# A second buffer for the convolved x, B and C tile in the projection phase of a hybrid attention/SSD layer

## The chip, the cores and the metric

The kernel runs on one core of a Trainium2 chip. The metric is the device time of one execution in microseconds (us), as the median of several runs. Before the change it is 2937.35 us, the median of 3 runs that lie between 2936.06 and 2943.05 us.

## What is computed

One step of a streaming encoder layer, for 2048 new prompt frames and 32 frames of a running stream. Only the mixer matters here. It projects the normalised input once, and reads attention (q, k, v) and a Mamba-2 SSD branch (z, x/B/C, dt) out of that projection:

```python
proj = h @ p['w_in']                      # q, k, v, z, xbc, dt_raw
xbc_c, conv_new = causal_dwconv(xbc, conv_prev, p['ssm_conv_w'], p['ssm_conv_b'])   # width 4
xbc_c = jax.nn.silu(xbc_c)
# x, B, C are parts of xbc_c
y, h_fin = ssd_scan(xh, dt, a, bm, cm, ssm_h0)
y = y + d_skip[:, None] * xh
y = rmsnorm(y * jax.nn.silu(z), p['g_ssm_out'])
out = jnp.concatenate([rmsnorm(attn, p['g_attn_out']), y], axis=-1) @ p['w_out']
```

A gated feed-forward network with a causal convolution of its own follows. Everything is float32 in and out; the matrix products are made from split operands (a high and a low part, three products).

## The kernel before

The features lie on the 128 partitions and the tokens along a row. The tokens are cut into four blocks (`SBS`): three of 512, and one of 544 that ends with the 32 frames of the running stream. The kernel has three parts: `phase_in` (phase one: all projections, the convolution and the SSD scan, block by block), then the attention, in which a stream of other work is interleaved with the heads, and with it the output projection and the feed-forward network.

One block `s` of phase one does, in the order of the source:

1. The normalised input is split into `xhi` and `xlo` (L315 to L323).
2. For each of the six column groups `c` of x, B and C (4 and 5 first, then 0 to 3), 24 matmuls (L161, by `dense`) fill a PSUM bank `o`, ScalarE copies it into the tile `raw` (L377, and L379 for the last 32 columns of the last block), and VectorE convolves it into the tile `xc`: one multiply-add with the bias (L384), three more taps (L388), then a sigmoid on ScalarE (L392) and a multiplication (L393).
3. The v projection (L412): 8 groups of 24 matmuls of 260 columns, whose banks ScalarE copies out into `v` (L419 in block 0, L421 after it). It needs no `xc`.
4. dt and its decays (L443 to L471), which go through memory once (`acD`) to be broadcast.
5. The SSD scan over 128 tokens at a time (L473 to L566). It reads `xc` as x, B and C and writes its result y over the x part of `xc` (L542, L545).
6. The next block's input is loaded and normalised (`prep`, L294 to L313), and k and q are projected (L573 to L594).
7. `gate` (L609) projects z and multiplies `xc` by silu(z) (L628, L630); `gate_norm` (L635) squares and sums `xc`, makes its reciprocal root (L180, L183), scales `xc` with it (L650), splits it into `khi` (L654, ScalarE) and `klo` (L656, GpSimd) and stores both. For the last block, steps 7 are not run here but as part of the stream beside the first attention heads.

So `xc` is taken at the head of a block and last read by L656 at the end of the block's step 7. Its pool `ssd_out` (opened in `build`, L1491) has one buffer, which the four blocks use in turn. The tile holds 6 x 547 float32 per partition, 13,128 bytes. `raw`, the input of the convolution, also has one buffer; the PSUM banks `o` (`psum_o`) are two, and the v projection, the x/B/C columns, k, q and z all use them.

Weights are made ready by `weight`: a DMA brings a piece (`wraw`), ScalarE writes its high part (L145), GpSimd subtracts that from it for the low part (L146). In phase one a piece is a whole group of 24 matmuls, and there are two buffers for it.

The order of the instructions on each engine isn't the source's. The framework (`schedule_with_timeline_sim=True`, L1616) orders them when the kernel is built: on a simulated time line, an engine takes the earliest instruction of the source whose inputs and buffers are ready by then. The order is then fixed. On the chip each engine works through its list, and an instruction that waits holds up what stands behind it on its engine.

Of the kernel before, what the change touches and what calls it, by code (L numbers as in the profile page):

```python
# [8 lines left out]
F32 = mybir.dt.float32  # L9
# [22 lines left out]
P = 128  # L32
# [220 lines left out]
def phase_in(kn, ctx):  # L253
# [101 lines left out]
    for s, (t0, nt) in enumerate(SBS):  # L355
# [5 lines left out]
            xs = split(s, nxt)  # L361
        xhi, xlo = xs
        raw = ep.tile([P, 6, 550], F32, name="raw")
        xc = kn.xcp.tile([P, 6, 547], F32, name="xc")
        W = 547 if last else 512
        nc.vector.tensor_copy(raw[:, :, 0:3], hist[:])
        if last:
# [233 lines left out]
        bufs = {"khi": 2, "klo": 2, "t": 2, "sq": 1}  # L601
# [870 lines left out]
def build(nc, tc, a, o):  # L1472
    kn = Kernel(nc, tc, a, o)
    with ExitStack() as ctx:
# [17 lines left out]
        with ExitStack() as c2:  # L1492
            kn.wp, kn.unit, kn.wbufs, kn.rbufs = c2.enter_context(tc.tile_pool(name="weights_in", bufs=1)), KC, 2, 2
            rest = phase_in(kn, c2)
# [125 lines left out]
```

## Time and profile before

| | |
|---|---|
| median of 3 runs | 2937.35 us |
| the profiled execution | 2941.02 us |
| its span (first to last instruction) | 2939.2 us |
| PE (TensorE matmul) busy | 2814.1 us, 96% of the span |
| DVE (VectorE) | 1690.8 us, 58% |
| ACT (ScalarE) | 1263.4 us, 43% |
| POOL (GpSimd) | 1275.4 us, 43% |
| granted TensorE clock, mean | 0.982 |
| first and last convolution step (L384) | 38.1 and 534.7 us from the span's start |

Names in a row of the profile are those of the program: `o L161` is the instruction of line 161 that writes a tile named `o`, and `out<-in` says what it writes and reads. PEld is TensorE's weight load, which overlaps the matmuls. In a list of waits, "A <- B: total, times, longest" says for how long A's engine sat idle until B released it. In a timeline, a row has its start and its length in us, the engine, the line, the operation, and how many instructions were merged; the bracket behind it is the idle time before it and what ended that.

### The profile page before, as it was taken

The numbers are of one execution on the slowest core, as the hardware profiler recorded it, in microseconds if no ns is written. First come the engines' busy times: TensorE is split into PE (matmuls) and PEld (weight loads), VectorE is DVE, ScalarE is ACT, GpSimd is POOL, SyncE is SP. The second block draws the span as 40 slices with busy tenths as digits, with TensorE's granted clock in tenths as the row PEclk, the third lists the DMA queues.
The fourth block names the chain that finished last, engine by engine and source line by source line (L and its number), as shares of the span: only waits on it lengthen the run. The fifth ranks groups of instructions, "written<-read, shape, count | busy, mean of one in ns | idle before, by whom it ended". The sixth has DMA issues, their size and how long they took to land.

```text
span 2939.2 us, 46252 instructions
## 1 busy us (share of the span) xinstructions
PE 2814.1 (96%) x16771; PEld 2427.5 (83%) x16771; DVE 1690.8 (58%) x2628; ACT 1263.4 (43%) x2622; POOL 1275.4 (43%) x1131
## 2 busy tenths in 40 slices
PE   7999999989889999999999999999999999999997
PEld 6777777977788888897788888977888889999997
DVE  7667586566773555447555556675666653623333
ACT  4344444337665555446333444654444443321111
POOL 4565555435766666656322323453223233511113
PEclk9999999989999999999999999999999999999999
DMA  5646464648787778777655556656555445765556
GB/s 179 183 137 193 132 176 124 174 115 271 247 282 263 253 263 276 266 256 250 215 180 172 174 180 219 225 182 205 176 172 170 160 159 202 241 181 179 170 178 200
DMA packets 333093, 586.47 MB, mean 200 GB/s; under 512 B 73306, under 2 KB 192738, under 8 KB 332866
## 3 DMA queue, kind: packets, MB, share of 16 engines
q1 hardware_dynamic: 332866, 583.52, 62.1%
q8 instruction: 134, 2.20, 0.3%
q14 instruction: 93, 0.76, 0.1%
HBM read 445.70 MB, written 137.69 MB: 198 GB/s over the span
## 4 chain that ended last, share of the span: by engine, by line
PE 72%; DVE 13%; DMA 7%; ACT 3%; issue 2%; POOL 1%; SPq 1%; DVEq 0%; ACTq 0%; POOLq 0%
PE o L161 35%; PE u L161 12%; PE t L161 10%; PE z L863 4%; PE pa L904 4%; PE pt L882 3%; DVE xc L388 2%; DMA acB<-acD 2%; PE o L412 1%; DVE acB L488 1%; DVE prow L714 1%; DMA xr<-hS 1%; DVE xc L384 1%; DVE xlo L320 1%; DVE x L310 1%
## 5 line engine op out<-in xcount | busy, mean ns | idle before, releaser
L161 PE MATMUL o<-xhi,w 128*128 128x512 f32 (+2 forms) x3968 | 1047.9, 346 | 24.1 <-ACT xhi L334 8.0
L161 PEld LDWEIGHTS o<-xhi,w 128*128 128x128 f32 x3968 | 697.3, 191 | 119.0 <-ACT xhi L334 8.0
L161 PE MATMUL o<-xlo,w 128*128 128x512 f32 (+2 forms) x1984 | 683.8, 345 | 6.3 <-DVE xlo L320 4.2
L146 POOL TENSOR_TENSOR w<-wraw,w 128x512 fp32r<-128x512 f32 (+3 forms) x244 | 384.3, 1577 | 261.4 <-ACT w L145 232.2
L719 POOL TENSOR_TENSOR beta<-beta,prow 128x512 f32<-128x512 f32 (+3 forms) x256 | 252.5, 987 | 442.7 <-DVE prow L714 366.8
L161 PEld LDWEIGHTS o<-xlo,w 128*128 128x128 f32 x1984 | 380.0, 192 | 50.4 <-DVE xlo L320 6.1
L161 PE MATMUL u<-xhi,w 128*128 128x512 f32 x1056 | 350.3, 398 | 0.0
L161 PE MATMUL o<-ah,w 128*128 128x512 f32 x992 | 344.4, 403 | 4.3 <-DVE f L1348 3.8
L1300 POOL TENSOR_TENSOR y<-y,gb 128x512 f32<-128x512 f32 (+1 forms) x88 | 116.0, 1318 | 503.2 <-ACT gb L1299 503.1
L714 DVE TENSOR_TENSOR_SCAN prow<-gam,prow,z 128x513 f32<-128x513 f32 x192 | 245.2, 1278 | 74.1 <-ACT beta L712 69.7
L887 DVE TENSOR_TENSOR wt<-pt,wt 128x512 fp32r<-128x512 f32 (+2 forms) x320 | 191.0, 602 | 159.6 <-ACT wt L886 157.8
L886 ACT CAST wt<-pt 128x512 fp32r<-128x512 f32 (+2 forms) x320 | 166.9, 527 | 218.2 <-PE pt L882 216.3
L145 ACT CAST w<-wraw 128x512 fp32r<-128x512 f32 (+3 forms) x244 | 172.1, 705 | 170.6 <-PE o L161 98.6
L161 PEld LDWEIGHTS u<-xhi,w 128*128 128x128 f32 x1056 | 199.1, 189 | 46.8
L161 PEld LDWEIGHTS o<-ah,w 128*128 128x128 f32 x992 | 187.2, 189 | 47.0 <-DVE f L1348 6.0
L711 ACT ACTIVATE gam<-z 128x512 f32<-128x512 f32 (+2 forms) x320 | 172.3, 538 | 96.0 <-PE z L863 53.9
L161 PE MATMUL u<-xlo,w 128*128 128x512 f32 x528 | 209.5, 397 | 0.0
L161 PE MATMUL o<-al,w 128*128 128x512 f32 x496 | 196.7, 397 | 0.0
L161 PE MATMUL t<-xhi,w 128*128 128x272 f32 x960 | 189.6, 293 | 2.6 <-DMA w<-wS_up 1.7
L882 PE MATMUL pt<-ident,beta 128*128 128x128 f32 x1088 | 180.3, 277 | 4.2 <-DVE wt L887 2.7
L1292 DVE SCALAR_TENSOR_TENSOR y<-gb,cv,y 128x512 f32<-128x512 f32 (+1 forms) x176 | 142.4, 809 | 72.6 <-ACT y L1290 69.9
L904 PE MATMUL pa<-wt,v 128*64 128x256 f32 (+3 forms) x1152 | 172.3, 280 | 8.6 <-DVE wt L887 6.6
(275 smaller groups left out, 4956.4 us busy)
## 6 DMA issues: line engine op xcount, KB each, us to landing
w<-wS_up SPq DMA_DIRECT2D x264, 512.0 KB, 3.6
w<-wS_dn SPq DMA_DIRECT2D x144, 384.0 KB, 3.5
wS_up<-w SPq DMA_DIRECT2D x88, 512.0 KB, 3.4
w<-wS_out SPq DMA_DIRECT2D x78, 512.0 KB, 5.7
wraw<-wup SPq DMA_DIRECT2D x88, 256.0 KB, 4.0
k<-kS SPq DMA_DIRECT2D x80, 256.0 KB, 4.1
v<-vS SPq DMA_DIRECT2D x80, 256.0 KB, 3.8
wS_dn<-w SPq DMA_DIRECT2D x48, 384.0 KB, 3.1
```

The costliest lines, as they stand in the source:

```text
L145: nc.scalar.copy(hi, raw[:, :m, :])
L146: nc.gpsimd.tensor_tensor(lo, raw[:, :m, :], hi.bitcast(F32), op=ALU.subtract)
L161: mm = nc.tensor.matmul(ps[:, : c1 - c0], l, r, start=first and i == 0 and k == 0, stop=last and i == 2 and k == len(w) - 1, **({"skip_gro ...
L711: nc.scalar.activation(g[:, c0:512], z, AF.Sigmoid, scale=-0.125)
L714: nc.vector.tensor_tensor_scan(back(pr), back(g), z[:, 0:1].to_broadcast([P, n + 1]), self.kn.ones[:, 0:1] if prev is None else prev, op0= ...
L719: eng.tensor_tensor(b[:, :n], b[:, :n], pr[:, c0 + 1 : 513], op=ALU.mult)
L863: mm = nc.tensor.matmul(z[:, :n], q[:, P * b : P * b + P], k[:, :n], start=e == 0, stop=e == 1 and kc < s)
L882: mm = nc.tensor.transpose(t[:, P * j : P * j + P], w[:, P * j : P * j + P], kn.ident[:])
L886: nc.scalar.copy(hi, t)
L887: nc.vector.tensor_tensor(lo, t, hi.bitcast(F32), op=ALU.subtract)
L904: nc.tensor.matmul(av[:m, 2 * P * p + c0 : 2 * P * p + 2 * P], v[:, j, :m], wt[:, rest, j, c0:], start=kc == s and p + j + rest == 0, stop ...
L1292: nc.vector.scalar_tensor_tensor(y[:, :W], gb[:, i : i + W], kn.col(wc + i), y[:, :W], op0=ALU.mult, op1=ALU.add)
```

## The change

The tile `xc` is asked for with two buffers in place of one. Nothing else is edited.

```diff
@@ -361,7 +361,7 @@
             xs = split(s, nxt)
         xhi, xlo = xs
         raw = ep.tile([P, 6, 550], F32, name="raw")
-        xc = kn.xcp.tile([P, 6, 547], F32, name="xc")
+        xc = kn.xcp.tile([P, 6, 547], F32, name="xc", bufs=2)
         W = 547 if last else 512
         nc.vector.tensor_copy(raw[:, :, 0:3], hist[:])
         if last:
```

## The prediction

> **What bounds the kernel now.** I read the page's first part, then the three stretches in which a block hands over to the next, then the waits.
>
> ```profile
> span 2939.2 us, 46252 instructions
> PE 2814.1 (96%) x16771; PEld 2427.5 (83%) x16771; DVE 1690.8 (58%) x2628; ACT 1263.4 (43%) x2622; POOL 1275.4 (43%) x1131
> ```
>
> TensorE is the bound: 96% of 2939.2 us. A change elsewhere can gain only where it removes idle time of PE. The three handovers (block 0 to 1, 1 to 2, 2 to 3), with PE's busy time first behind the length:
>
> ```profile
> 140.00:250.00 110.00, 104.56 (x560) 86.48 (x560) 74.11 (x97) 49.34 (x76) 68.47 (x40) 0.99 0.48 144
> 290.00:420.00 130.00, 119.60 (x625) 97.93 (x626) 80.64 (x112) 55.93 (x87) 71.63 (x43) 0.96 0.45 135
> 455.00:590.00 135.00, 127.37 (x897) 116.84 (x896) 80.55 (x116) 56.94 (x100) 65.95 (x43) 0.99 0.52 146
> ```
>
> PE is idle for 5.4, 10.4 and 7.6 us there, 23.4 together. That is all that these stretches can give, and only part of it hangs on `xc`. First the wait for `xc` among VectorE's waits up to 660 us, then PE's own:
>
> ```profile
> DVE xc L384 <- POOL klo L656: 18.4, 3, 7.1
> ```
>
> ```profile
> PE o L412 <- ACT v L421: 8.9, 3, 3.4
> ...
> PE o L161 <- DVE t L628: 5.1, 2, 2.6
> ...
> PE o L161 <- DVE xlo L320: 4.2, 3, 1.8
> ...
> PE o L412 <- ACT v L419: 3.2, 2, 2.3
> ...
> PE o L412 <- ACT raw L377: 1.7, 1, 1.7
> ...
> PE o L412 <- ACT raw L379: 0.9, 1, 0.9
> PE o L161 <- ACT sq L641: 0.9, 1, 0.9
> PE z L762 <- DMA qp<-qF: 0.8, 1, 0.8
> ```
>
> The wait that the change removes is the row L384 <- klo L656: 18.4 us in three pieces, the convolution of a block standing until the previous block's last reader of `xc` is done. It is idle time of VectorE. What reaches PE is the row L412 <- L421, 8.9 us, one piece per handover. How the one leads to the other is in the timelines of the first handover, ScalarE, then VectorE, then GpSimd:
>
> ```profile
> 182.99 0.57 ACT L377 COPY raw<-o 128x512 f32<-128x512 f32 x1
> ...
> 205.01 0.59 ACT L377 COPY raw<-o 128x512 f32<-128x512 f32 x1 [0.16 <-PE o L161]
> 205.49 1.06 ACT L145 CAST w<-wraw 128x1024 fp32r<-128x1024 f32 x1
> 210.66 0.59 ACT L377 COPY raw<-o 128x512 f32<-128x512 f32 x1 [4.11 <-PE o L161]
> ...
> 223.34 1.29 ACT L392 ACTIVATE t<-xc 128x512 f32<-128x512 f32 x2 [5.28 <-DVE xc L388]
> 224.54 0.63 ACT L421 COPY v<-o 128x260 f32<-128x260 f32 x2
> ```
>
> ```profile
> 193.83 3.35 DVE L183 RECIPROCAL rstd<-rstd 128x512 f32<-128x512 f32 x1 [11.42 <-ACT rstd L180]
> 197.22 4.63 DVE L650 SCALAR_TENSOR_TENSOR xc<-xc,cv,rstd 128x512 f32<-128x512 f32 x4
> 207.49 4.44 DVE L384 TENSOR_SCALAR xc<-raw,cv 128x512 f32<-128x512 f32 x5 [5.64 <-POOL klo L656]
> 211.85 4.72 DVE L388 SCALAR_TENSOR_TENSOR xc<-raw,cv,xc 128x512 f32<-128x512 f32 x7
> 216.49 2.63 DVE L384 TENSOR_SCALAR xc<-raw,cv 128x512 f32<-128x512 f32 x1
> ```
>
> ```profile
> 207.42 2.40 POOL L146 TENSOR_TENSOR w<-wraw,w 128x1024 fp32r<-128x1024 f32 x1
> 212.28 6.56 POOL L146 TENSOR_TENSOR w<-wraw,w 128x1024 fp32r<-128x1024 f32 x1 [2.46 <-ACT w L145]
> ```
>
> The first column of `raw` is there at 183.56 us, the sixth at 211.25, but the first convolution step starts at 207.49. All six columns are then worked off in one pile. ScalarE stands for 5.28 us at a sigmoid (L392) that waits for the convolution, and behind it stand the copies L421 that empty the v banks. With two banks, PE waits. So the chain is: last reader of `xc`, pile of convolutions, sigmoid, bank copy, PE.
>
> **What is removed.** At most the v waits of the three handovers, 8.9 us, and the 0.9 us of L379, which occurs in the last block alone and is of the same kind: 9.8 us. The other waits in the list stay, since their producers (L628 of `gate`, the split L320, the square L641) run before `xc` is asked for again. After the v projection PE has k and q matmuls to fill the scan, so I let a us that is gained there reach the end.
>
> Whether it is all gained needs VectorE's new timetable. The durations (shortest/median/longest) of the convolution:
>
> ```profile
> L388 DVE SCALAR_TENSOR_TENSOR xc<-raw,cv,xc x72: 736/744/2920, 42.7 to 542.9; 128x512 f32<-128x512 f32 x54, 128x547 f32<-128x547 f32 x18
> ...
> L384 DVE TENSOR_SCALAR xc<-raw,cv x24: 532/540/2645, 38.1 to 534.7; 128x512 f32<-128x512 f32 x18, 128x547 f32<-128x547 f32 x6
> L392 ACT ACTIVATE t<-xc x24: 629/632/667, 51.8 to 543.8; 128x512 f32<-128x512 f32 x18, 128x547 f32<-128x547 f32 x6
> L393 DVE TENSOR_TENSOR xc<-xc,t x24: 678/686/1814, 54.3 to 544.5; 128x512 f32<-128x512 f32 x18, 128x547 f32<-128x547 f32 x6
> ```
>
> A column costs VectorE 0.54 + 3 x 0.744 + 0.686 = 3.46 us, six cost 20.8. With the reciprocal (3.35) and the four L650 (4.63), which still come in between, that is 28.8 us of work from 183.56 on: 212.4 if nothing waited. The last column only arrives at 211.25, so it ends near 211.25 + 3.46 + 0.63 = 215.3. The copy that was late is that of the third v group. The groups start when the x/B/C matmuls end, near 210.5 (the last L377 starts at 210.66), and a copy at 224.54 made PE wait about 3 us, so it was wanted by about 221. The sigmoids then are through with some 5 us to spare. Each time a convolution step meets GpSimd it is lengthened by 2 us (L384 above took 2.63 where its median is 0.54), and two or three of these eat the margin. So I don't take the wait as gone. The bounds: nothing left, or as much as in block 0, where `xc` is free from the start and PE still waited 3.2 us for L419 and 1.7 for L377, 4.9 us. Block 0 has extra VectorE work in that place (the split of the v weights, the scaling by `r0`), so I take a value near the low end: 0.9 us a handover, the smallest wait of this kind in the list. That is 2.7 us left of the 9.8.
>
> **What is added.** No instruction. But the convolution moves from after the x/B/C matmuls to beside them, where PE needs a new piece of weights for each group. A group lasts 5.65 us (L377 at 205.01, then at 210.66). When one ends, ScalarE copies the bank (0.59) and casts a piece (1.06), GpSimd subtracts (2.40): 4.05 us, so the piece is ready 1.6 us before it is wanted. Two things can use that up.
>
> First, a sigmoid now stands among the casts on ScalarE. Queued behind it: the bank copies, the casts, and by them GpSimd's L146 and PE. It costs 0.63 us where its input is ready, inside the 1.6.
>
> Second, GpSimd's L146 and VectorE's L388 don't run together. In the rows above L146 took 6.56 us in place of 2.40 exactly while seven L388 ran back to back (211.85 to 216.57), then L384 took 2.63 while L146 finished. A late L146 did no harm there, since PE was at the v projection, which has its own weights. Now it can. One column by itself: the bank copy ends at 0.59 after the group, L384 at 1.13, three L388 at 4.72 / 7 = 0.67 each by 3.15; L146 is ready at 1.65 and waits 1.5, which just fits into 1.6. Two columns in a pile, as after the reciprocal and L650 have held VectorE for 8.0 us: a delay of up to 6.56 - 2.40 = 4.16, so PE waits 4.16 - 1.6 = 2.6 us. From 0 to 2.6 us for each of five pieces in three handovers, 0 to 39 us; I take half of one such wait per handover, 1.3 us, because a pile can form at one place only: 3.9 us. A gain is excluded for this term, since nothing leaves GpSimd.
>
> [...]
>
> The second buffer also moves what is laid out beside it. The first tiles of the next stage that might now wait for space are those of the running stream, and PE waited 0.8 us there for their data (L762). I take 0 and keep 1 us each way.
>
> Sum: 9.8 - 2.7 - 3.9 = 3.2 us gained. The profiled execution, 2941.02 us (1.8 of it outside its span), would come to 2937.8; it lies 3.7 above the median of the runs, so I take 3.2 from 2937.35: **2934.2 us**.
>
> **Rivals.** A measurement of this kernel can tell 0.3%, 8.8 us: below 2928.5 counts as faster, above 2946.2 as slower.
>
> *All of it is gained.* The sigmoids never hold the v copies, and L146 stays inside its slack: 9.8 us, 2927.6. For it speaks VectorE's idle 11.42 us right where the first columns arrive; against it, block 0.
>
> *Block 0 repeats itself.* The order on ScalarE is fixed beforehand, and if it counts on a faster VectorE, a sigmoid stands before a v copy as it did there: 3 x 4.9 = 14.7 in place of 9.8, a loss of 4.9, 2942.3. This is also the case in which the change does nothing for PE: one wait has taken the place of another.
>
> *Weights late, slower.* The mechanism is the exclusion of L146 and L388 at the x/B/C groups. It decides once the 15 pieces are late for PE by more than 9.8 us together, 0.65 each, and it passes the measurable bound at 18.6, 1.24 each. At 1.5 us each it gives 22.5 - 9.8 = 12.7 slower, 2950. For it: L146 at 6.56 us, and GpSimd which in this stretch also has the `klo` subtractions of L656; against it: the columns arrive 5.65 us apart and cost VectorE 3.46, so piles should be rare. [...]
>
> **How the numbers follow.** The forecast (part of the wait gone, a little lost on weights) has a chance of 0.50; all gained 0.20; block 0 again 0.15; weights late 0.15. Faster by over 0.3%: nearly the whole of the second case, 0.19, its rest being within the bound. Slower: 0.15. Within 0.3%: 0.66. The range goes from 2926 (all gained, and the 1 us of the layout) to 2950 (1.5 us a piece); its two tails, a better new order than I see and a worse one, get 0.2 together. The forecast's own range is 2928.5 to 2940.
>
> **What would show it.** In the changed kernel L384 <- L656 is gone from the waits, and the convolution's first step starts within a us or two of the first L377 of its block. If the step of the v waits is right, L412 <- L421 falls from 8.9 to about 3 us. If the step on weights is right, a row PE o L161 <- POOL w L146 of a few us appears, with long L146 rows beside runs of L388. If PE's idle time in the three stretches falls by much more than 9.8, or time changes after 660 us, the order of other work has changed, which I haven't counted, and the prediction is wrong.

## The result and the profile after

The changed kernel takes 2957.08 us (median of 5 runs, 2951.90 to 2964.86); the kernel before, run beside it, 2937.35 us (5 runs, 2934.03 to 2943.14). The ratio is 1.0064, 95% interval 1.004 to 1.0087. It is slower, by about 19 us, and lies above the range. The profiled execution took 2953.76 us, 12.7 more than that of before.

The page of the changed kernel, first part:

```profile
span 2952.0 us, 46252 instructions
PE 2816.8 (95%) x16771; PEld 2430.1 (82%) x16771; DVE 1713.6 (58%) x2628; ACT 1262.5 (43%) x2622; POOL 1276.4 (43%) x1131
```

The instructions are the same in number, and PE is busy for 2.7 us more in a span that is 12.8 longer: so most of the loss is PE standing idle. Where? The same three handovers as in the prediction, changed kernel (PE's busy time and the granted clock are what to compare):

```profile
140.00:250.00 110.00, 99.49 (x525) 81.94 (x524) 77.57 (x92) 45.49 (x71) 59.84 (x36) 0.97 0.44 133
290.00:420.00 130.00, 122.61 (x663) 100.55 (x661) 91.95 (x120) 58.65 (x91) 80.00 (x47) 1.00 0.51 153
455.00:590.00 135.00, 126.60 (x886) 116.03 (x886) 84.80 (x114) 54.79 (x97) 66.06 (x42) 0.97 0.50 141
```

PE's idle time there was 5.4, 10.4 and 7.6 us and is now 10.5, 7.4 and 8.4: worse, better, a little worse. What that comes to at the end of phase one is read from the start of the first score matmul of the attention (L863), and the last start of the same line tells the end of the attention. First the kernel before, then the changed one (columns: line, engine, operation, tiles, count; shortest/median/longest ns; first and last start in us):

```profile
L863 PE MATMUL z<-k,qa x320: 220/475/796, 646.3 to 2406.8; 128*128 128x512 f32 x96, 128*128 128x128 f32 x32, 128*128 128x384 f32 x32
```

```profile
L863 PE MATMUL z<-k,qa x320: 221/475/796, 644.4 to 2420.6; 128*128 128x512 f32 x96, 128*128 128x128 f32 x32, 128*128 128x384 f32 x32
```

Phase one ends 1.9 us **earlier**; the attention ends 13.8 us **later**. The last instruction that reads `xc` is an L656 beside the first heads, at 779 us. Following each matmul's start against that of before (the n-th matmul of a line and tile against its counterpart, the median in steps of 20 us), the changed kernel is 0.4 us early at 780, 1 to 5 us late at 900 to 1280 us, 7 at 1300, 14 to 16 at 1360 to 1400, up to 26 at 1460, then levels off at about 18 from 1600 to 1920 and at about 14 from 2000 us on. (Where the order differs, single values jump.) So the loss comes into being after the last instruction that touches `xc`. The stretch from 1280 to 1500 us is where the attention heads of one block give way to the next while the feed-forward of block 0 is being finished. Before, then after:

```profile
1280.00:1500.00 220.00, 211.09 (x1233) 181.30 (x1232) 129.28 (x198) 106.23 (x252) 106.06 (x116) 0.99 0.69 226
```

```profile
1280.00:1500.00 220.00, 199.70 (x1182) 173.26 (x1181) 129.63 (x195) 103.21 (x245) 104.09 (x115) 0.95 0.67 221
```

PE loses 11.4 us of busy time and the granted clock falls from 0.99 to 0.95; fewer matmuls get done. An estimate from these rows: 0.04 of 220 us is some 9 us of clock, 20 us with the idle time; the shift grows by 19 us there, from 3.8 at 1280 to 23 at 1500. PE's waits in that stretch, changed kernel:

```profile
PE z L863 <- DVE rn_v L220: 5.4, 1, 5.4
PE o L161 <- DVE f L1348: 4.7, 3, 3.5
PE o L161 <- ACT f L1346: 2.9, 1, 2.9
```

The first isn't there before; L1348 held PE for 1.8 us in two waits there and L1346 for 0.2. The longest wait of before in this stretch, which the changed kernel hasn't, was:

```profile
PE u L238 <- POOL rn_v L226: 3.5, 1, 3.5
```

VectorE's timeline shows how the first of the changed kernel arises:

```profile
1425.55 0.42 DVE L1384 TENSOR_TENSOR f<-f,xr 128x256 f32<-128x256 f32 x1 [5.92 <-DMA xr<-hS]
1425.89 0.69 DVE L1313 TENSOR_TENSOR y<-u,y 128x512 f32<-128x512 f32 x1
1429.25 1.50 DVE L1384 TENSOR_TENSOR f<-f,xr 128x256 f32<-128x256 f32 x1 [2.68 <-DMA xr<-hS]
1430.67 0.68 DVE L1279 TENSOR_TENSOR gb<-o,r 128x512 f32<-128x512 f32 x1
1431.28 1.27 DVE L714 TENSOR_TENSOR_SCAN prow<-gam,prow,z 128x513 f32<-128x513 f32 x1
1432.46 0.13 DVE L220 SCALAR_TENSOR_TENSOR rn_v<-u,rcol 128x2 f32<-128x2 f32 x1
```

L1384 is the last addition of the feed-forward. It needs a piece of the residual, `xr`, which SyncE loads into one of two buffers (L1379) after the earlier piece has been used and its sum queued for the store (L1385). While VectorE stands there for 5.92 and 2.68 us, the scan L714 of the attention and the L220 behind it stand too, and PE can't start the next scores until 1432.60 us. The code around L1379 to L1384 is the same in both kernels. What differs is the order. Counted from the two traces (line, operation and tiles of each matmul, equal neighbours taken together), PE's lists have some 10,080 rows; set side by side they differ in 515, 65 of them before the first L863 and nearly all the rest between 640 and 2000 us, in the attention. The order is worked out on a simulated time line when the kernel is built, so an earlier phase one can move that time line under all that follows; the simulated times themselves are not shown here.

Phase one itself did not go as forecast either. PE's waits from 100 to 640 us, changed kernel:

```profile
PE o L412 <- ACT raw L377: 10.5, 4, 4.1
PE o L161 <- POOL w L146: 4.6, 9, 0.7
...
PE y L498 <- DVE xc L393: 3.4, 1, 3.4
PE o L161 <- DVE t L628: 3.0, 2, 2.5
...
PE o L412 <- ACT v L421: 1.5, 1, 1.5
```

The v copies L421 no longer hold PE (8.9 us before, 1.5 now), but the copies L377 do, 10.5 us, in the first two handovers (5.9 and 4.6 us). In the third PE stands for neither, but its first scan matmul there (L498) waits 3.4 us for a convolved column, which it did not before. ScalarE, then VectorE, then PE, at the first handover:

```profile
212.78 0.63 ACT L392 ACTIVATE t<-xc 128x512 f32<-128x512 f32 x1 [4.47 <-DVE xc L388]
213.32 0.60 ACT L654 CAST khi<-xc 128x512 fp32r<-128x512 f32 x1
214.23 0.63 ACT L392 ACTIVATE t<-xc 128x512 f32<-128x512 f32 x1 [0.31 <-DVE xc L388]
214.77 0.57 ACT L377 COPY raw<-o 128x512 f32<-128x512 f32 x1
215.24 1.05 ACT L145 CAST w<-wraw 128x1024 fp32r<-128x1024 f32 x1
221.50 0.63 ACT L392 ACTIVATE t<-xc 128x512 f32<-128x512 f32 x1 [5.21 <-DVE xc L388]
222.03 0.57 ACT L377 COPY raw<-o 128x512 f32<-128x512 f32 x1
```

```profile
181.71 0.55 DVE L384 TENSOR_SCALAR xc<-raw,cv 128x512 f32<-128x512 f32 x1 [1.18 <-ACT raw L377]
182.29 6.17 DVE L388 SCALAR_TENSOR_TENSOR xc<-raw,cv,xc 128x512 f32<-128x512 f32 x3
```

```profile
215.39 0.39 PE L412 MATMUL o<-wvhi,xhi 128*128 128x260 f32 x1 [1.78 <-ACT raw L377]
...
222.66 0.59 PE L412 MATMUL o<-wvhi,xhi 128*128 128x260 f32 x1 [4.12 <-ACT raw L377]
```

The convolution starts 25.8 us earlier than before (181.71 instead of 207.49 us). But three L388 took 6.17 us, and the next sigmoid in ScalarE's fixed list now stands **ahead** of the copy that empties a bank. So ScalarE waits 4.47 and 5.21 us for the convolution, and behind it a copy L377 is late for PE. Before, ScalarE had worked off its copies L377 first. The means of all L388 of 512 columns, before, then after (busy us, mean ns):

```profile
L388 DVE SCALAR_TENSOR_TENSOR xc<-raw,cv,xc 128x512 f32<-128x512 f32 x54 | 47.2, 925 | 0.0
```

```profile
L388 DVE SCALAR_TENSOR_TENSOR xc<-raw,cv,xc 128x512 f32<-128x512 f32 x54 | 64.9, 1220 | 0.8
```

### The profile page after: what moved, and what is told of

The parts are those of the page before. It is cut to its first block, busy times and chain, and to the rows that moved or that the text cites. A ratio compares the mean times of both kernels' runs of the same rounds, so it can differ in the third digit from the quotient of the medians.

```text
span 2952.0 us, 46252 instructions
## 1 busy us (share of the span) xinstructions
PE 2816.8 (95%) x16771; PEld 2430.1 (82%) x16771; DVE 1713.6 (58%) x2628; ACT 1262.5 (43%) x2622; POOL 1276.4 (43%) x1131
## 4 chain that ended last, share of the span: by engine, by line
PE 67%; DVE 4%; DMA 3%; ACT 2%; issue 1%; POOL 1%; SPq 0%; DVEq 0%; POOLq 0%; ACTq 0%
PE o L161 31%; PE u L161 12%; PE t L161 11%; PE z L863 4%; PE pa L904 4%; PE pt L882 3%; DVE prow L714 1%; DMA xr<-hS 1%; DVE xlo L1052 1%; PE u L203 1%; DMA w<-wS_out 0%; DMA sk<-ck 0%; PE u L238 0%; DVE f L1380 0%; DVE wt L887 0%
## 5 line engine op out<-in xcount | busy, mean ns | idle before, releaser
L161 PE MATMUL o<-xhi,w 128*128 128x512 f32 (+2 forms) x3968 | 1052.0, 346 | 26.8 <-ACT xhi L334 7.9
L161 PEld LDWEIGHTS o<-xhi,w 128*128 128x128 f32 x3968 | 699.2, 192 | 123.8 <-POOL w L146 9.8
L161 PE MATMUL o<-xlo,w 128*128 128x512 f32 (+2 forms) x1984 | 683.5, 345 | 5.2 <-DVE xlo L1052 2.0
L146 POOL TENSOR_TENSOR w<-wraw,w 128x512 fp32r<-128x512 f32 (+3 forms) x244 | 382.9, 1571 | 279.6 <-ACT w L145 257.3
L161 PEld LDWEIGHTS o<-xlo,w 128*128 128x128 f32 x1984 | 380.6, 192 | 48.8 <-DVE xlo L1052 2.9
L161 PE MATMUL o<-ah,w 128*128 128x512 f32 x992 | 344.8, 404 | 9.8 <-DVE f L1348 6.8
L161 PE MATMUL u<-xhi,w 128*128 128x512 f32 x1056 | 348.7, 397 | 0.0
L714 DVE TENSOR_TENSOR_SCAN prow<-gam,prow,z 128x513 f32<-128x513 f32 x192 | 245.3, 1278 | 59.3 <-ACT beta L712 56.3
L145 ACT CAST w<-wraw 128x512 fp32r<-128x512 f32 (+3 forms) x244 | 171.9, 705 | 170.0 <-PE o L161 109.7
L161 PEld LDWEIGHTS u<-xhi,w 128*128 128x128 f32 x1056 | 198.7, 188 | 46.7
L161 PEld LDWEIGHTS o<-ah,w 128*128 128x128 f32 x992 | 187.6, 189 | 52.2 <-DVE f L1348 8.3
L161 PE MATMUL u<-xlo,w 128*128 128x512 f32 x528 | 209.3, 396 | 0.0
L161 PE MATMUL o<-al,w 128*128 128x512 f32 x496 | 197.1, 397 | 0.0
L161 PE MATMUL t<-xhi,w 128*128 128x272 f32 x960 | 189.3, 293 | 3.0 <-DMA w<-wS_up 1.5
L904 PE MATMUL pa<-wt,v 128*64 128x256 f32 (+3 forms) x1152 | 171.4, 279 | 11.2 <-DVE wt L887 10.4
```

The costliest lines, as they stand in the source:

```text
L145: nc.scalar.copy(hi, raw[:, :m, :])
L146: nc.gpsimd.tensor_tensor(lo, raw[:, :m, :], hi.bitcast(F32), op=ALU.subtract)
L161: mm = nc.tensor.matmul(ps[:, : c1 - c0], l, r, start=first and i == 0 and k == 0, stop=last and i == 2 and k == len(w) - 1, **({"skip_gro ...
L714: nc.vector.tensor_tensor_scan(back(pr), back(g), z[:, 0:1].to_broadcast([P, n + 1]), self.kn.ones[:, 0:1] if prev is None else prev, op0= ...
L904: nc.tensor.matmul(av[:m, 2 * P * p + c0 : 2 * P * p + 2 * P], v[:, j, :m], wt[:, rest, j, c0:], start=kc == s and p + j + rest == 0, stop ...
```

## The experiments

All but one of the kernels hold part of the order while the buffers vary. The program is first scheduled with `ORDER_OF` buffers, and the list of each engine is read from it; then it is built with `BUFS` buffers, and for the part named in `SCOPE` each instruction of an engine is made to follow its neighbour in that list. "Early" is what phase one issues, "late" what comes after it. No instruction is added and no wait is taken away. The lines of `BUFS` below are shortened, and behind each stands the name of its run. Common to all of them:

```diff
-        xc = kn.xcp.tile([P, 6, 547], F32, name="xc")
+        xc = kn.xcp.tile([P, 6, 547], F32, name="xc", bufs=kn.xbufs)
...
+            for names in keep.values():
+                for p, n in zip(names, names[1:]):
+                    tc.add_manual_dep(by[n], p, info, reason="order")
```

Each was timed beside the kernel before on the same chip, in 6 to 12 runs, and ratios are against that: its median was 2939.08 us (35 runs) for the first four, 2937.06 (22 runs) for the next three, 2936.46 (11 runs) for the last. Times after 660 us are shifts against the profile of before, found as above.

**Is it the later order?** The two halves apart: first, two buffers with the later work in the order of before; then one buffer with the later work in the order of the changed kernel.

```diff
+BUFS, ORDER_OF, SCOPE = 2, 1, "late"      # late1_b2
+BUFS, ORDER_OF, SCOPE = 1, 2, "late"      # late2_b1
```

> Two buffers, phase one ordered as in the changed kernel; everything that the source has behind phase one is held to the order that it has with one buffer. Theory A (the loss is made by the new order of the later work, at about 1290 to 1480 us): phase one keeps its small gain, the k/q matmuls of the attention start some 1.9 us earlier than before, and the time is 2935 us, 2931 to 2940. Theory B (the loss is made in phase one, by the second buffer and the new waits there, and only shows later): as the changed kernel, 2952 to 2962 us.

> One buffer, phase one ordered as before; the work behind phase one is held to the order that it gets with two buffers. Theory A: the whole loss is there without the second buffer, 2957 us, 2951 to 2963. Theory B: 2937 us, 2933 to 2941.

Measured: late1_b2 2940.05 us, ratio 1.0001 (0.9987 to 1.0015); late2_b1 2951.88 us, ratio 1.0047 (1.003 to 1.0064). So a kernel with a single `xc` buffer, whose phase one keeps the old order, has most of the loss, and the kernel with two buffers but the old later order has none. In one thing theory A missed: the small gain of phase one isn't kept in late1_b2, whose first L863 starts at 646.7 us, 0.4 us later than before. The two ratios together make 1.0048, inside the interval of the changed kernel. In the profile of late2_b1 the waits are those of the changed kernel, in the same stretch, 1280 to 1500 us, PE first, then VectorE:

```profile
PE z L863 <- DVE rn_v L220: 5.3, 1, 5.3
PE o L161 <- DVE f L1348: 4.7, 3, 3.5
```

```profile
DVE f L1384 <- DMA xr<-hS: 16.4, 6, 5.4
```

The first half is settled as well: in late1_b2, phase one with two buffers is worth nothing. Its PE waits from 100 to 640 us show why, the copies L377 and the weights again:

```profile
PE o L412 <- ACT raw L377: 8.9, 4, 3.1
PE o L161 <- POOL w L146: 4.9, 8, 1.2
```

**Does any change upstream do that?** A change in phase one that has nothing to do with `xc`, with one buffer and nothing held: q is projected before k, which reorders the later work too.

```diff
-        for name, dst in (("wk", kn.kS), ("wq", kn.qS)):
+        for name, dst in (("wq", kn.qS), ("wk", kn.kS)):
```

> One buffer; in phase one the q columns are projected before the k columns (the two passes of the loop at L573 are exchanged). The same work, no wait taken away, but the order of much of the later work changes. Theory A: such a change of order moves the time by several us either way, mainly between 640 and 1640 us, 2930 to 2960. Theory B: nothing comes of it, 2933 to 2941.

Measured: 2943.13 us, ratio 1.001 (0.9992 to 1.0029): not told apart from no change. Its profiled execution is 9 us late at 1500 us and 6.6 at the end. So not every reordering costs 14 us; the size belongs to the particular order. That reorderings in general scatter by some us is suggested by this profile, but one run isn't enough to show it.

**What does phase one hold back?** Two buffers, with phase one as a whole in its old order; and two buffers with only ScalarE in its old order, so that VectorE convolves early, beside the x/B/C matmuls, while the sigmoids stay behind the copies. In both the later work has the old order (in the first it came out so by itself: PE's list in its trace differs from that of before in 2 rows).

```diff
+BUFS, ORDER_OF, SCOPE = 2, 1, "early"                                     # early1_b2
+BUFS, ORDER_OF, SCOPE = 2, 1, {"early": ("Activation",), "late": <all>}   # act1_b2
```

> Two buffers, but phase one held to the order that it has with one; the rest then gets its old order too. The wait of L384 for L656 goes, nothing moves beside the x/B/C matmuls. Theory A: the convolution starts about 5 us earlier in each handover, right behind L650, so the v waits of PE (8.9 us) go down to 2 or less with nothing added: 2930 us, 2926 to 2935. Theory B: if the second buffer costs by itself (its place in memory), slower than 2941.

> Two buffers for xc, all later work in its old order; in phase one only ACT is held to its old order, the others are free. The convolution then runs beside the x/B/C matmuls as in the changed kernel, but its sigmoids stay behind them. Theory P (in phase one the new waits come from the sigmoids L392 that now stand ahead of the copies L377 on ACT): the waits L412 <- L377 (10.5 us) go, those for L421 do not come back, 2926 to 2933 us. Theory Q (they come from L146 and L388 excluding each other): the waits for POOL w L146 stay at about 5 us or grow and the time is that of the changed phase one, 2936 to 2943 us.

Measured: early1_b2 2931.92 us, ratio 0.9976 (0.996 to 0.9991); act1_b2 2921.16 us, ratio 0.9948 (0.9929 to 0.9967). The first score matmul L863 starts at 639.4 and 630.2 us in their profiles, 646.3 before, 644.4 in the changed kernel, 646.7 in late1_b2. The second buffer by itself, with nothing reordered, is therefore a small gain (its profiled execution, 2939.3 us, was the slowest of its 12), and with VectorE free to start early a larger one. Neither came just as expected: in early1_b2 L421 still holds PE for 4.5 us in three waits, not 2 or less, and act1_b2 is faster than theory P's range. PE's waits of act1_b2 from 100 to 640 us, and ScalarE at its first handover:

```profile
PE o L161 <- POOL w L146: 3.1, 4, 1.0
...
PE o L412 <- ACT v L421: 2.2, 1, 2.2
PE st L532 <- DVE hT L562: 2.1, 2, 1.6
PE o L161 <- ACT raw L377: 0.9, 1, 0.9
```

```profile
210.81 0.59 ACT L377 COPY raw<-o 128x512 f32<-128x512 f32 x1 [4.96 <-PE o L161]
...
213.68 0.38 ACT L421 COPY v<-o 128x260 f32<-128x260 f32 x1 [1.33 <-PE o L412]
216.53 0.38 ACT L421 COPY v<-o 128x260 f32<-128x260 f32 x1 [2.47 <-PE o L412]
...
218.22 1.15 ACT L392 ACTIVATE t<-xc 128x512 f32<-128x512 f32 x2
```

The row of 10.5 us, L412 <- L377, is gone. ScalarE now waits for PE, not PE for ScalarE, and the sigmoids come when their inputs are long there. VectorE's L388 are as slow as in the changed kernel (mean 1198 ns); that they are slow costs little here, where no bank copy is queued behind a sigmoid that waits for them. What was held is the whole list of ScalarE, not the sigmoids alone, and the free engines settled into other lists than in late1_b2 (118 rows of PE's and 78 of VectorE's differ in the traces); how much of the gain is the sigmoids' place alone stays open. act1_b2 beats both kernels, that of before by 15.9 us and the changed one by some 34 us going by the two ratios.

**What in the later order costs?** The suspect is the wait L1384 <- `xr`. Six `xr` buffers in place of two, with SyncE's queue left free so that the loads may run ahead; in the later order of the changed kernel, and in the old one.

```diff
-                h = att.tmp.tile([P, 272], F32, name="xr", bufs=2)[:, :n]
+                h = att.tmp.tile([P, 272], F32, name="xr", bufs=6)[:, :n]
...
+BUFS, ORDER_OF, SCOPE = 2, 2, {"early": <all>, "late": <all but SP>}   # late2_xr6
+BUFS, ORDER_OF, SCOPE = 2, 1, {"early": <all>, "late": <all but SP>}   # early1_xr6
```

> The changed kernel with six in place of two buffers for the tile xr, which brings the residual of the previous block for the last addition of the feed-forward network (L1374). PE, DVE, ACT and POOL keep the order of the changed kernel, SP may issue the loads earlier. Theory A (the later loss comes from DVE additions L1384 that wait for xr<-hS, 16.4 us at 1380 to 1500 us, with a scan L714 or a copy that PE needs queued behind them): the PE wait of 5.4 us for z L863 and those of 1.2 us (L203) and 2.9 us (L1346) go, and with them the half-clock slices near 1440 us; 8 to 14 us less than the changed kernel, 2943 to 2950 us. Theory B (the loss is in the order on PE itself): still 2951 to 2962 us.

> Two buffers for xc, phase one and the later work in their old order on PE, DVE, ACT and POOL, and six buffers for xr with SP free to load it earlier. Theory A: DVE's waits for xr<-hS (13.5 us at 1360 to 1480 us in the kernel before) go, PE lost only about 3.5 us by them there: 2927 to 2932 us. Theory B: no difference from the same kernel with two xr buffers, 2930 to 2935 us.

Measured: late2_xr6 2939.54 us, ratio 1.0007 (0.999 to 1.0024); early1_xr6 2926.41 us, ratio 0.996 (0.9946 to 0.9974). With the `xr` loads ahead, the changed kernel's order is not measurably slower than the kernel before; that is more than theory A gave it (2943 to 2950). PE's waits and the window of late2_xr6, 1280 to 1500 us:

```profile
PE o L161 <- DVE f L1348: 4.7, 3, 3.5
...
PE z L863 <- DVE rn_v L220: 0.8, 1, 0.8
```

```profile
1280.00:1500.00 220.00, 208.65 (x1249) 180.61 (x1247) 133.17 (x203) 109.45 (x258) 108.91 (x117) 0.99 0.71 233
```

The 5.4 us are down to 0.8, no wait for `xr` is left on VectorE, the clock is back at 0.99 and 9 of the 11.4 us of PE's time with it. The f L1348 row stays: it has another cause (in the changed kernel, four L1052, 3.96 us from 1373.55 us on, stand ahead of one L1348 on VectorE), which the buffers don't touch.

In the old order the same edit moved the ratio from 0.9976 to 0.996, 4.7 us, with intervals that overlap; its median lies just under theory A's range. In the new order it is 1.0064 to 1.0007 from the changed kernel, which differs from late2_xr6 in this edit alone, some 17 us (1.0047 from late2_b1, 11.8 us). The traces say the same of the stretch from 1280 to 1500 us: the edit gives PE 3.5 us more of busy time in the old order (211.24 in early1_b2, 214.77 in early1_xr6; PE's wait L238 <- L226 falls from 3.3 to 0.3 us) and 9.0 in the new one. So the wait for `xr` costs more in the new order than in the old one, but not all of it belongs to the new order. The free SyncE queue was not tried with two buffers, so the two halves of this edit aren't told apart.

**Both gains together.** Held ScalarE and six `xr` buffers:

```diff
+BUFS, ORDER_OF, SCOPE = 2, 1, {"early": ("Activation",), "late": <all but SP>}   # act1_xr6, xr 6 buffers
```

> Two changes of the earlier kernels together: two buffers for xc with ScalarE held to its old order in phase one (15.9 us under the kernel before by itself), and six buffers for xr beside the later work in its old order, with SyncE's queue left free (5.5 us between the two kernels that differ in it alone). If the two gains lie in different stretches and the order after 660 us decides by itself what xr costs, they add up: 2937 - 15.9 - 5.5, near 2916, with VectorE's wait L1384 <- xr near zero between 1280 and 1500 us. If the wait for xr is hidden once phase one ends earlier, or the free queue of SyncE shifts phase one, nothing is added: 2919 to 2923.

Measured: 2920.09 us (2915.62 to 2928.44), ratio 0.995 (0.9931 to 0.9969). The wait for `xr` is gone from VectorE's list and the profiled execution, at 2916.41 us, is 4.5 under that of act1_b2, but the ratios of the two don't differ. In the old later order `xr` buffers are worth nothing that could be measured here on top of act1_b2, so of the two expectations it is the second that came.

## Why the prediction was wrong

**The step that failed** is "I let a us that is gained there reach the end". The prediction costed phase one and passed its result on to the end unchanged. It did say that a change after 660 us would mean that "the order of other work has changed, which I haven't counted", but it gave that no term and no rival, though it names for "block 0 repeats itself" that the order is fixed beforehand; only the tails of its range, "a better new order than I see and a worse one", have a chance, 0.2 together. Measured by itself (late2_b1), that missing term is +0.47% (0.3 to 0.64), about +14 us, and it is most of the result (+0.64%, 0.4 to 0.87). It came from a place some 700 us behind the last convolution.

**The wait that goes, and the convolution's start**: right. L384 <- L656 is gone from VectorE's list, and at the first handover the first step starts when its L377 ends.

**The v waits, 9.8 us with 2.7 left**: L421 fell from 8.9 to 1.5 us, but L412 <- L377 took its place with 10.5. The 9.8 became 12.0, so this step gave a loss of 2.2 us where 7.1 of gain were counted, and the new wait L498 <- L393 is another 3.4. That is near the mechanism of the rival "block 0 repeats itself", at 0.15, with a smaller price than its 14.7. Two parts of its working failed. A column was costed at 3.46 us of VectorE from medians (L388 744 ns, where even before the mean was 925); beside GpSimd's work (L146, but also L645 and L656) the mean became 1220 ns, and "two or three of these" meetings was too few. And the copies thought to be at risk were the v copies at the end of the pile; those at risk were the x/B/C copies within it. The timelines show the sigmoid waiting ahead of the copy, and act1_b2 bears it out: with ScalarE's old list, sigmoids behind the copies, the 10.5 us vanish, though the convolution is just as slow.

**Weights, 3.9 us**: about the right size, by another way, which is luck in part. L161 <- L146 went from 1.3 us in two waits to 4.6 in nine, 3.3 us more. There was no pile, but small waits, 0.7 us the longest: six at x/B/C groups of the first two handovers, 2.9 us together, and three at the k and q projections. The longest L146 took 3.02 us, not 6.56; VectorE paid instead, in its L388 (mean 1220 ns in place of 925). One of the six came by a way that the prediction hadn't: the cast L145 (189.57 us) stood on ScalarE behind a sigmoid that had waited 5.41 us for the convolution. L146 was delayed by 0.61 us at most (3.02 less 2.41), not by the 4.16 that I had taken from the row of 6.56 us; that is within the slack of 1.6 us that I had worked out, and PE waited all the same.

**The layout, 0**: right as far as the runs tell. early1_b2 has the two-buffer layout with the old order and is faster.

**The ceiling, 9.8 us**: too low. act1_b2 gains 15.9 us, and its matmuls are already 16 us early at 630 us, all in phase one. The waits that went account for 6.7 (L421), 0.9 (L379) and 2.5 (L532 <- L562, 4.6 to 2.1 us), against 1.8 more for the weights; some of the rest may be clock (590 to 660 us: granted 0.85 before, 0.90 in act1_b2, though that window holds somewhat later work there). The remaining us are not assigned.

**The net of phase one**: forecast −3.2 us, measured 1.0001 (late1_b2), −1.9 us in the profile of the changed kernel. This error is small, but by luck: the two terms by themselves came to losses of 2.2 and 3.3 us, and what made up for them are waits that the prediction held unchanged, among them L161 <- L628 (5.1 to 3.0 us) and L161 <- L320 (4.2 to 1.6). What shortened those stays open. What remains unsettled is the rest of the loss in the later order beyond the `xr` wait: the f L1348 row (2.9 us over before) is one candidate that wasn't tried by itself.

## What to carry to other kernels

Where the order of instructions is worked out on a simulated time line, an edit has two effects: its own, and that of the new order it gives to everything behind it. Hold the old order of the later work to measure the first, and price the second as a risk of either sign. And when a buffer lets an engine start earlier, look at what is now queued behind the instruction that waits for that engine: in this kernel, with the later order held in both, keeping ScalarE's old list, with the sigmoids behind the bank copies, turned no gain (1.0001) into some 15 us (0.9948). Shallow load buffers can be cheap in one order and costly in another: the edit on `xr` gave PE 3.5 us in one and 9.0 in the other.

## What the runs showed of the hardware

One wait of PE was followed by slow matmuls, a loss beyond its length. Right around that wait of 5.36 us, the changed kernel's window reads (its last three figures are the granted clock, the DMA share and GB/s):

```profile
1430.00:1438.00 8.00, 3.33 (x13) 2.96 (x14) 6.75 (x9) 4.45 (x9) 3.55 (x4) 0.50 0.74 245
```

The granted clock is 0.50 for these 8 us, and 0.95 in the 13 us behind them; from 1425 to 1428 us it is 1.00, and again from 1440 to 1442. So the matmuls right behind the wait ran at half clock (an L863 of 512 columns on `qb` took 0.63 us at 1433.19 and 0.39 at 1439.50). That the wait brought the clock down is my reading; what brings it down and up again is not shown. Through the stretch from 1280 to 1500 us the clock is 0.95 in place of 0.99. The prediction counted waits at their length only, for gain and loss alike.

The second is L388 beside GpSimd. Three in a row took 6.17 us (182.29 to 188.46) against 2.2 for three at the median of before, and what GpSimd did meanwhile is not L146 alone; L645 adds up the squares for the norm, and the prediction didn't count it:

```profile
180.56 2.87 POOL L645 TENSOR_TENSOR sq<-sq,t 128x512 f32<-128x512 f32 x2 [3.70 <-ACT t L644]
183.38 2.84 POOL L146 TENSOR_TENSOR w<-wraw,w 128x1024 fp32r<-128x1024 f32 x1
186.18 1.74 POOL L645 TENSOR_TENSOR sq<-sq,t 128x512 f32<-128x512 f32 x1
```

L146 was at 2.51 us (median from 140 to 600 us) against 2.41 before. Here GpSimd was at work when the first L388 came. In the row of 6.56 us of before, the L388 were (from 211.85 us, L146 from 212.28), and GpSimd was the one delayed. Which of the two pays turned round, and the price of 4.16 us taken from the one row did not hold in the other. What decides it is not shown: from 190.41 us three L388 took 4.33 us, the first of them ahead of an L146 (from 190.69 us), and that L146 took 2.71.
